# A hybrid diffusion step on one core: the gate's strips of two weight quarters put in a row, and the last norm's root taken from ScalarE's own sum

## The chip, the core and the metric

The kernel runs on one core of a Trainium2 chip. Its five engines work side by side, each through its own instructions in order: TensorE (PE, with its weight loads shown apart as PEld), VectorE (DVE), ScalarE (ACT), GpSimd (POOL) and SyncE (SP), whose queue here issues most of the DMA transfers. They wait for each other by semaphores. The metric is the device time of one execution in microseconds (us), the median of several runs.

## The reference

One layer of a diffusion trunk, in fp32, over 1024 latent tokens and 128 context tokens (nine tiles of 128 rows), 1024 wide:

```python
def _rmsnorm(x, g):
    y = x * lax.rsqrt(jnp.mean(x * x, axis=-1, keepdims=True) + EPS)
    return y * g
...
    mod = jax.nn.silu(cond) @ w_ada + b_ada
    shift, scale, gate = jnp.split(mod[:, None, :], 3, axis=-1)
    h = _rmsnorm(x, norm_g) * (1 + scale) + shift
    u, v, g_a, c_q, c_kv, k_rope, g_b = _split_in(h @ w_in)
    a_out = _chunk_mlp(u, v, w_s, b_s, g_v) * jax.nn.silu(g_a)
...
    y = jnp.concatenate([a_out, attn * jax.nn.silu(g_b)], axis=-1) @ w_o
    return x + gate * y
...
    y_prompt = _rmsnorm(xp, final_g)
    y_sample = _rmsnorm(xs, final_g)
```

Two places of it matter here: `gate`, the last third of the modulation (two conditions, latent and context, by 1024 columns, a product of two vectors of 1024 with a 1024 x 1024 part of w_ada, plus a bias), and the last `_rmsnorm`, of the ninth tile (the context tokens).

## The kernel before, in words

fp32 products are made of three passes over a high and a low part (fp32r) of each operand. The stages follow each other on PE almost without a gap: modulation and transposes; the wide input projection (u, g_a and g_b as six pairs n = 0 to 5 of column blocks, each pair in seven half-size products p1 to p7 by a Strassen-like scheme, and plain products tp of 24 matmuls for the third group of tokens); the narrow projection; attention; the output projection, also by such a scheme, in which the norm of each tile follows as its rows are done.

The order of the input projection's instructions comes from a small planner (class `Plan`): each step has an engine, a cost, what it depends on, a priority and resources, and the planner issues steps on a clock of its own. What it issues stands so on each engine; the time on the chip is then set by data and semaphores. A step on "D" issues DMAs on SP's queue.

The gate is made in the middle of this, at pair 3, in four quarters j of 256 columns (`gate_steps`):

- `ga{j}` fetches 1 MB of weights (`adag`, one buffer) and 2 KB of bias (`grow`).
- `gr{j}`, the strips: eight matmuls with 32 columns of weights (the two conditions and zeros), four of them side by side in four strips of the array, L1014. They write columns 0 to 255 of a PSUM bank `gps{j}` (`pst`, two banks).
- `gh{j}` and `gl{j}`: ScalarE takes the high part, DVE the low part.
- `gt{j}`, the sum: two small matmuls (L1026) add the four strips into columns 256 to 511 of the same bank.
- `go{j}`: DVE adds the bias, and SP writes the quarter to DRAM (`gdram`), from which the gate is loaded some 320 us later.

Where the strips and sums stand among PE's products is given by their dependencies on product steps, such as `"p3_2"`. Only when a quarter's strips are done may the next quarter's weights be fetched, as they share the buffer.

The last norm (`finish_left`) is that of tile 8, whose left half is PE's last product, in two parts of 256 columns. The squares of the right half and of the first part are summed early; `zv1` makes of them a mean with the epsilon. ScalarE squares the second part with an accumulated sum (`zq`); DVE joins the two (`zv`, L2327), ScalarE takes the root (`zr`, L2328), DVE makes minus a half of the mean square (`zw`, L2329), the reciprocal of the root (`zr0`) and a Newton step (`zr2`, `zr3`); then three engines scale the two halves and two DMAs write them. The small values lie in one PSUM bank, `smalls`.

Of the kernel before, what the change touches and what calls it, by code (L numbers as in the profile page):

```python
# [9 lines left out]
F32 = mybir.dt.float32  # L10
# [3 lines left out]
AF = mybir.ActivationFunctionType  # L14
ALU = mybir.AluOpType
# [3 lines left out]
P = 128  # L19
# [4 lines left out]
EPS = 1e-6  # L24
# [70 lines left out]
def tile_hymba_step(ctx: ExitStack, tc: tile.TileContext, I, O):  # L95
    nc = tc.nc
    V, S, G, T = nc.vector, nc.scalar, nc.gpsimd, nc.tensor

    def opened(name, bufs=1, space=None, side=None):
        kw = dict(name=name, bufs=bufs, reuse_waits="tile")  # L100
        if space is not None:
            kw["space"] = space
        if side is not None:
            kw["side"] = side
        cm = tc.tile_pool(**kw)
        return cm, cm.__enter__()
# [4 lines left out]
    def lo_of(lo, src, hi):  # L111
        V.tensor_tensor(lo, src, f32(hi), op=ALU.subtract)  # L112
# [58 lines left out]
    def catch_up(until):  # L171
        at_ = now[0]
        while waiting and waiting[0][0] <= until:
            due, fn = waiting.pop(0)
            now[0] = due
            fn()
        now[0] = at_
# [9 lines left out]
    def step(cost, fn):  # L187

        catch_up(now[0])
        for f in list(fill):  # L190
            if f[0] in made and made_at[f[0]] <= now[0]:
                fill.remove(f)
                run(f[1:])
        run((cost, fn))
# [12 lines left out]
    def run(step):  # L207
        catch_up(now[0])
        step[1]()
        now[0] += step[0]  # L210
# [16 lines left out]
    c_pc, pc = opened("pc", side="right")  # L227
    c_mx, mx = opened("mx", side="right")
    c_mc, mc = opened("mc", side="right")
    c_sm, sm = opened("sm", bufs=2, side="right")  # L230
    c_pt, pst = opened("pst", bufs=2, space=PSUM)
# [131 lines left out]
    ada = {}  # L363
# [276 lines left out]
    step = plan.add  # L640

    def bank(pool, tag, name):
        return pool.tile([P, 512], F32, tag=tag, name=name)
# [28 lines left out]
    def load_step(key, fn, deps, prio, cost=1.46):  # L672
        step(key, "D", cost, fn, deps, prio, lag=2.0)
# [81 lines left out]
    pools, opened_as = {}, {}  # L755
# [242 lines left out]
    def gate_steps(j):  # L998


        cell = {}
        prio = 8 + 0.1 * j

        def fetch():
            cell["w"] = pools["vg"].tile([P, 8, 256], F32, tag="ada", name=f"adag{j}")
            nc.sync.dma_start(cell["w"], I["ada_g"][j])
            cell["row"] = pools["vg"].tile([2, 256], F32, tag="row", name=f"grow{j}", bufs=2)
            nc.sync.dma_start(cell["row"], I["b_gate"][j : j + 1, :].rearrange("a (c r) -> (a c) r", c=2))

        def strips():  # L1010
            cell["ps"] = bank(pst, "t", f"gps{j}")
            for kk in range(NK):
                s_, i = kk % 4, kk // 4
                T.matmul(cell["ps"][32 * s_ : 32 * s_ + 32, 0:256], csp[:, kk, :], cell["w"][:, kk, :], start=i == 0, stop=i == 1)  # L1014

        def high():
            cell["hi"] = pools["vg"].tile([P, 256], F32R, tag="hig", name=f"hig{j}")
            S.copy(cell["hi"], cell["ps"][:, 0:256])

        def low():  # L1020
            cell["lo"] = pools["vg"].tile([P, 256], F32R, tag="log", name=f"log{j}")
            lo_of(cell["lo"], cell["ps"][:, 0:256], cell["hi"])

        def total():
            for m in range(2):
                T.matmul(cell["ps"][0:2, 256:512], selr, cell[("hi", "lo")[m]], start=m == 0, stop=m == 1)  # L1026

        def out():
            V.tensor_tensor(cell["row"], cell["ps"][0:2, 256:512], cell["row"], op=ALU.add)
            nc.sync.dma_start(gdram[:, 256 * j : 256 * j + 256], cell["row"])  # L1030

        load_step(f"ga{j}", fetch, ["vg", *([f"gr{j - 1}"] if j else [])], prio, cost=3.6)
        step(f"gr{j}", "T", 0.7, strips, [f"ga{j}", ("p3_2", "tp62", "p1_3", "p6_3")[j]], 4.0, takes=("pst",))
        step(f"gh{j}", "S", 0.4, high, [f"gr{j}"], 1.0)
        step(f"gl{j}", "V", 0.4, low, [f"gh{j}"], 1.0)
        step(f"gt{j}", "T", 0.35, total, [f"gl{j}", ("tp62", "p1_3", "p2_3", "p7_3")[j]], 4.0)
        step(f"go{j}", "V", 0.35, out, [f"gt{j}"], 1.0, gives=("pst",))

    def wide_weights():

# [78 lines left out]
    wuv = pc.tile([P, 4, P], F32, tag="wuv", name="wuv")  # L1119
# [444 lines left out]
    def pair_scores(i):  # L1564

        return score_steps(*heads[i]) if FROM <= i < UPTO else [s_ for h in range(2) for s_ in plain_steps(*heads[i + h])]
# [245 lines left out]
    with tc.manual_schedule(engines=engines):  # L1812
# [168 lines left out]
        first = pair_scores(0)  # L1981
# [76 lines left out]
    gate, ssq = {}, {}  # L2058
# [3 lines left out]
    step = plan.add  # L2062
    L, R = slice(0, 512), slice(512, 1024)

    def on_v(key, fn, deps, prio, cost=0.64, **kw):
        step(key, "V", cost, fn, deps, prio, lag=0.12, **kw)

    def on_s(key, fn, deps, prio, cost=0.6, **kw):
        step(key, "S", cost, fn, deps, prio, lag=0.15, **kw)
# [38 lines left out]
    def small(n):  # L2108
        c = used[0]
        used[0] += n  # L2110
        return smalls[:, c : c + n]
# [62 lines left out]
    for q in range(3, len(queue)):  # L2174
        n, name, _ = queue[q]
        cell = {}
# [16 lines left out]
    turn = [None]  # L2193
# [99 lines left out]
        product(2, first_banks[2], ks=[3])  # L2293

    def finish_left():
        v, v0, root, u, vn = (small(1) for _ in range(5))
        r = sm.tile([P, 1], F32, tag="fr", name="rlast")
        cell = {}
        fetch("own0", lambda: load_own(0, nc.sync.dma_start), ["y4"])
        g, x = (lambda: own[0][:, 0:512]), (lambda: own[0][:, 512:1024])  # L2300
        on_g("z4", lambda: G.tensor_tensor(keep, keep, fg[:, R], op=ALU.mult), ["sq8.1", "fg"], 2.5)

        cut_at = 256
        own_of = (slice(0, cut_at), slice(cut_at, 512))
        at_ = (slice(0, cut_at), slice(0, 512 - cut_at))

        def left(j):
            cell[j] = psw.tile([P, 512], F32, tag="w", name=f"left{j}")
            if j == 0:
                cell["junk"] = psw.tile([P, 512], F32, tag="w", name="junk")  # L2310
            out_terms(8, cell[j][:, at_[j]], own_of[j].start, own_of[j].stop, range(8))

        for j in range(2):
            o = lambda j=j: cell[j][:, at_[j]]
            dur = 0.43
            on_t(f"pz{j}", 2.9, lambda j=j: left(j), [], takes=("w",) if j else ("w", "w"))
            on_v(f"zm{j}", lambda o=o, c=own_of[j]: V.tensor_tensor(o(), o(), g()[:, c], op=ALU.mult), [f"pz{j}", "own0"], 0.5, dur)
            on_v(f"za{j}", lambda o=o, c=own_of[j]: V.tensor_tensor(o(), o(), x()[:, c], op=ALU.add), [f"zm{j}"], 0.5, dur)
        square(8, 0, lambda: cell["junk"][:, own_of[0]], L, ["za0"], 0.5, lambda: cell[0][:, own_of[0]])
        sums((8,), v0, 0.5)  # L2320
        on_v("zv1", lambda: V.tensor_scalar(v0, v0, 1.0 / 1024.0, EPS, op0=ALU.mult, op1=ALU.add), ["n8"], 0.5, 0.16)
        on_s(
            "zq", lambda: S.activation(cell["junk"][:, own_of[1]], cell[1][:, at_[1]], AF.Square, accum_out=ssq[(8,)][:, 2:3]), ["za1"], 0.4, 0.5
        )
        first, second = own_of
        on_v("zf", lambda: V.tensor_tensor(x()[:, first], cell[0][:, at_[0]], fg[:, first], op=ALU.mult), ["sq8.0", "fg"], 0.6, 0.43)
        on_v("zv", lambda: V.scalar_tensor_tensor(v, ssq[(8,)][:, 2:3], 1.0 / 1024.0, v0, op0=ALU.mult, op1=ALU.add), ["zq", "zv1"], 0.4, 0.2)  # L2327
        on_s("zr", lambda: S.activation(root, v, AF.Sqrt), ["zv"], 0.3, 0.25)  # L2328
        on_v("zw", lambda: V.tensor_scalar(vn, v, -0.5, None, op0=ALU.mult), ["zv"], 0.3, 0.16)  # L2329
        on_v("zr0", lambda: V.reciprocal(r, root), ["zr"], 0.2, 0.18)  # L2330
        on_v("zr2", lambda: V.scalar_tensor_tensor(u, r, r, vn, op0=ALU.mult, op1=ALU.mult), ["zr0", "zw"], 0.3, 0.18)
        on_v("zr3", lambda: V.scalar_tensor_tensor(r, u, 1.5, r, op0=ALU.add, op1=ALU.mult), ["zr2"], 0.3, 0.18)

        def out0():
            G.tensor_scalar(x()[:, first], x()[:, first], r, 0.0, op0=ALU.mult, op1=ALU.add)
            V.scalar_tensor_tensor(x()[:, second], cell[1][:, at_[1]], r, fg[:, second], op0=ALU.mult, op1=ALU.mult)
            nc.sync.dma_start(O["y"][8][:, L], x())

        def out1():
            S.activation(keep, keep, AF.Copy, scale=r)  # L2340
            nc.scalar.dma_start(O["y"][8][:, R], keep)

        on_v("zo0", out0, ["zr3", "zf"], 0.3, 0.6)
        on_s("zo1", out1, ["zr3", "z4"], 0.3, 0.6)
# [109 lines left out]
```

## Time and profile before

| what | value |
| --- | --- |
| runs | 602.42, 601.96, 602.82 us |
| median | 602.42 us |
| the profiled execution's own time | 602.15 us |
| its span, first to last instruction | 600.4 us |
| PE busy | 590.3 us (98%) |
| DVE, ACT, POOL busy | 427.3, 329.2, 214.0 us |
| mean granted TensorE clock | 0.997 |
| strips of the four quarters, starts on PE | 162.48, 170.21, 177.90, 185.62 us |

A row of a timeline has the start, the duration, the engine, the line, the operation, what it writes and reads, and a count; equal instructions in a row are merged. In brackets stands the idle time of the engine ahead of it and what ended it ("issue" is nothing that the profile shows). Matmuls overlap, so a merged row's duration reaches past the start of the next; a difference of starts is the time that a piece takes.

### The profile page before, as it was taken

The page shows a single profiled execution, that of the slowest core. Times are in us where ns is not written, and L with a number is a line of the kernel's source. Part 1 is how long each engine was busy: PE and PEld are TensorE (multiplying, and loading weights), DVE is VectorE, ACT ScalarE, POOL GpSimd, SP SyncE. Part 2 cuts the span into 40 slices and gives each one's busy share as a digit, 9 for nine tenths or more (in the row PEclk, how much of TensorE's full clock was granted, in tenths as well). Part 3 has the DMA queues.
Part 4 walks back from the last instruction along what each step waited for, and adds up shares of the span by engine and source line. Part 5 has one row for each costly group of instructions (what it writes and reads, how often), then busy time and mean ns, then how long its engine had stood idle before and what let it go on. Part 6 is the DMA issues. An engine that isn't in the chain of part 4 may idle for free.

```text
span 600.4 us, 10191 instructions
## 1 busy us (share of the span) xinstructions
PE 590.3 (98%) x3661; PEld 528.2 (88%) x3661; DVE 427.3 (71%) x940; ACT 329.2 (55%) x773; POOL 214.0 (36%) x251
## 2 busy tenths in 40 slices
PE   9999999999999999999999999999999999999995
PEld 8578889999989999999998888888888898888884
DVE  4666888977647368476678677778788876477885
ACT  6565886434323245465577566656656462457543
POOL 2571103200000000343363345454544547269834
PEclk9999999999999999999999999999999999999998
DMA  8991001032052134100002033434242029951444
GB/s 319 370 370 70 1 2 70 1 140 71 4 212 69 69 93 138 43 1 0 2 8 71 0 106 106 157 126 141 81 143 94 1 72 303 361 178 41 144 147 160
DMA packets 31059, 67.33 MB, mean 112 GB/s; under 512 B 3344, under 2 KB 17440, under 8 KB 29984
## 3 DMA queue, kind: packets, MB, share of 16 engines
q1 hardware_dynamic: 27792, 55.93, 26.9%
q0 software_dynamic: 2352, 8.39, 4.1%
q10 hardware_dynamic: 864, 2.36, 1.1%
q8 instruction: 29, 0.48, 0.3%
q14 instruction: 22, 0.18, 0.1%
HBM read 53.45 MB, written 13.21 MB: 111 GB/s over the span
## 4 chain that ended last, share of the span: by engine, by line
PE 93%; DMA 3%; DVE 2%; ACT 1%; POOL 1%; issue 0%; SPq 0%; POOLq 0%; ACTq 0%
PE p L916 14%; PE tp L937 7%; PE pT L1586 6%; PE o L1610 3%; PE o L1612 3%; PE o L1611 3%; PE zacc L1349 2%; PE zacc L1348 2%; PE zacc L1350 2%; PE S L1947 2%; PE S L1948 2%; PE S L1949 2%; DMA ada<-in_ada_ss 2%; PE s L1503 2%; PE s L1506 2%; PE s L1505 2%
## 5 line engine op out<-in xcount | busy, mean ns | idle before, releaser
L1463 POOL TENSOR_SCALAR e<-e,rs 128x1280 f32<-128x1280 f32 x32 | 47.0, 1468 | 97.2 <-DVE rs L1462 62.8
L112 DVE TENSOR_TENSOR pl<-pT,ph 128x512 fp32r<-128x512 f32 x81 | 55.5, 687 | 32.5 <-ACT ph L1590 32.2
L1458 ACT ACTIVATE e<-s,nb,scl 128x256 f32<-128x256 f32 x64 | 56.9, 890 | 38.9 <-DVE nb L1446 26.2
L1590 ACT CAST ph<-pT 128x512 fp32r<-128x512 f32 x80 | 47.1, 589 | 40.8 <-PE pT L1586 40.6
L1196 POOL TENSOR_TENSOR kr<-z,rope 128x64 f32<-128x64 f32 x8 | 2.6, 324 | 155.3 <-ACT z L1205 155.3
L937 PE MATMUL tp<-area,w 128*128 128x384 f32 x288 | 52.6, 338 | 0.0
L1610 PE MATMUL o<-ph,vh 128*128 128x256 f32 x160 | 50.7, 317 | 0.0
L937 PEld LDWEIGHTS tp<-area,w 128*128 128x128 f32 x288 | 50.4, 188 | 0.0
L1586 PE MATMUL pT<-ident,e 128*128 128x128 f32 x320 | 48.0, 273 | 0.0
L1586 PEld LDWEIGHTS pT<-ident,e 128*128 128x128 f32 x320 | 38.9, 140 | 7.2
L1612 PE MATMUL o<-ph,vl 128*128 128x256 f32 x160 | 45.1, 282 | 0.0
L1611 PE MATMUL o<-pl,vh 128*128 128x256 f32 x160 | 44.9, 280 | 0.0
L1440 DVE TENSOR_REDUCE m<-s 128x1 f32<-128x1024 f32 x32 | 39.0, 1218 | 2.6 <-PE s L1481 2.5
L1610 PEld LDWEIGHTS o<-ph,vh 128*128 128x128 f32 x160 | 30.2, 189 | 4.7 <-ACT os L1620 2.9
L1611 PEld LDWEIGHTS o<-pl,vh 128*128 128x128 f32 x160 | 30.4, 190 | 0.4
L1612 PEld LDWEIGHTS o<-ph,vl 128*128 128x128 f32 x160 | 30.1, 188 | 0.0
L916 PE MATMUL p<-area,w 128*128 128x384 f32 x144 | 27.7, 339 | 0.0
L916 PE MATMUL p<-area,s 128*128 128x384 f32 x144 | 27.3, 337 | 0.0
L1348 PE MATMUL zacc<-w1t,area 128*128 128x448 f32 x72 | 27.1, 376 | 0.0
L916 PE MATMUL p<-w1t,s 128*128 128x384 f32 x144 | 26.9, 339 | 0.0
L1349 PE MATMUL zacc<-w1t,area 128*128 128x448 f32 x72 | 26.3, 366 | 0.0
L1350 PE MATMUL zacc<-w1t,area 128*128 128x448 f32 x72 | 26.3, 365 | 0.0
(697 smaller groups left out, 1770.4 us busy)
## 6 DMA issues: line engine op xcount, KB each, us to landing
ada<-in_ada_ss SPq DMA_DIRECT2D x16, 512.0 KB, 6.0
w2r<-in_w_t SPq DMA_DIRECT2D x12, 512.0 KB, 5.1
x<-in_x SPq DMA_DIRECT2D x9, 512.0 KB, 8.4
adag<-in_ada_g SPq DMA_DIRECT2D x4, 1024.0 KB, 4.8
traw<-in_w_o SPq DMA_DIRECT2D x16, 256.0 KB, 3.8
tdram<-thi SPq DMA_DIRECT2D x32, 128.0 KB, 1.9
tdram<-traw SPq DMA_DIRECT2D x32, 128.0 KB, 1.8
wor<-in_w_o SPq DMA_DIRECT2D x8, 512.0 KB, 3.8
```

What stands on the lines that cost most here:

```text
L112: V.tensor_tensor(lo, src, f32(hi), op=ALU.subtract)
L916: T.matmul(banks[key], a_, b_, start=k == 0 and m == 0, stop=k == 3 and m == len(passes) - 1)
L937: T.matmul(tps[c, 2][:, :GW], w_[c][:, k, :], x_[k, 2], start=k == 0 and m == 0, stop=k == NK - 1 and m == 2)
L1348: T.matmul(ps[:, :448], a, wqh[k], start=k == 0, stop=False)
L1440: V.tensor_reduce(m[:, 0:1], lat_, axis=AX.X, op=ALU.max)
L1458: S.activation(e[:, sl], src, AF.Exp, bias=nb, scale=scl[:, t : t + 1], accum_out=su[:, i : i + 1])
L1463: G.tensor_scalar(e, e, rs, 0.0, op0=ALU.mult, op1=ALU.add)
L1586: T.transpose(ps[:, w : w + P], es[t, h][:, c * P : (c + 1) * P], ident)
L1590: later(0.5, lambda: S.copy(ph[:, :w], ps[:, :w]))
L1610: T.matmul(o, vh[:, kt, :], ph[:, sl], start=c == 0, stop=False)
L1611: T.matmul(o, vh[:, kt, :], pl[:, sl], start=False, stop=False)
L1612: T.matmul(o, vl[:, kt, :], ph[:, sl], start=False, stop=c == n - 1)
```

## The change

Two separate edits.

**The gate.** Quarters 0 and 1 get their strips directly behind each other in the middle of p1 of pair 3, quarters 2 and 3 behind the plain product of the same pair. For this the weights have two buffers, quarter j's being fetched when the strips of quarter j - 2 are done. The biases are fetched by a step of their own and lie in a shared tile (`grows`, in the slot that `wuv` uses later), two halves in turn. High, low, sum and output remain four each; the high part of the second quarter of a couple waits for the first one's sum, with which it shares a buffer.

**The last norm.** The share of the other columns with the epsilon goes into `rest8` in SBUF; the root is taken straight from ScalarE's accumulated sum, with `rest8` as bias. DVE makes minus a half of `rest8` ahead of time (`zv2`), and the half of the mean square from this and the accumulated sum (`zw`).

```diff
--- before.py
+++ after.py
@@ -1002,10 +1002,8 @@
         prio = 8 + 0.1 * j
 
         def fetch():
-            cell["w"] = pools["vg"].tile([P, 8, 256], F32, tag="ada", name=f"adag{j}")
+            cell["w"] = pools["vg"].tile([P, 8, 256], F32, tag="ada", name=f"adag{j}", bufs=2)
             nc.sync.dma_start(cell["w"], I["ada_g"][j])
-            cell["row"] = pools["vg"].tile([2, 256], F32, tag="row", name=f"grow{j}", bufs=2)
-            nc.sync.dma_start(cell["row"], I["b_gate"][j : j + 1, :].rearrange("a (c r) -> (a c) r", c=2))
 
         def strips():
             cell["ps"] = bank(pst, "t", f"gps{j}")
@@ -1013,6 +1011,12 @@
                 s_, i = kk % 4, kk // 4
                 T.matmul(cell["ps"][32 * s_ : 32 * s_ + 32, 0:256], csp[:, kk, :], cell["w"][:, kk, :], start=i == 0, stop=i == 1)
 
+        def bias():
+            if j == 0:
+                pools["rows"] = pc.tile([P, 512], F32, tag="wuv", name="grows")
+            cell["row"] = pools["rows"][0:2, 256 * (j % 2) : 256 * (j % 2) + 256]
+            nc.sync.dma_start(cell["row"], I["b_gate"][j : j + 1, :].rearrange("a (c r) -> (a c) r", c=2))
+
         def high():
             cell["hi"] = pools["vg"].tile([P, 256], F32R, tag="hig", name=f"hig{j}")
             S.copy(cell["hi"], cell["ps"][:, 0:256])
@@ -1029,12 +1033,19 @@
             V.tensor_tensor(cell["row"], cell["ps"][0:2, 256:512], cell["row"], op=ALU.add)
             nc.sync.dma_start(gdram[:, 256 * j : 256 * j + 256], cell["row"])
 
-        load_step(f"ga{j}", fetch, ["vg", *([f"gr{j - 1}"] if j else [])], prio, cost=3.6)
-        step(f"gr{j}", "T", 0.7, strips, [f"ga{j}", ("p3_2", "tp62", "p1_3", "p6_3")[j]], 4.0, takes=("pst",))
-        step(f"gh{j}", "S", 0.4, high, [f"gr{j}"], 1.0)
+        first = j % 2 == 0
+        load_step(f"ga{j}", fetch, ["vg", *([f"gr{j - 2}"] if j > 1 else [])], prio, cost=3.0)
+        load_step(f"gb{j}", bias, [f"ga{j}", *([f"go{j - 2}"] if j > 1 else [])], prio, cost=0.6)
+        turn = ["p3_2", "p1_3"][j // 2]
+        if first:
+            waits = [f"ga{j}", f"ga{j + 1}", turn, *(["go1"] if j else [])]
+            step(f"gr{j}", "T", 0.85, strips, waits, 4.0, takes=("pst",))
+        else:
+            step(f"gr{j}", "T", 0.95, strips, [f"|gr{j - 1}"], 0, takes=("pst",))
+        step(f"gh{j}", "S", 0.4, high, [f"gr{j}", *([] if first else [f"gt{j - 1}"])], 1.0)
         step(f"gl{j}", "V", 0.4, low, [f"gh{j}"], 1.0)
-        step(f"gt{j}", "T", 0.35, total, [f"gl{j}", ("tp62", "p1_3", "p2_3", "p7_3")[j]], 4.0)
-        step(f"go{j}", "V", 0.35, out, [f"gt{j}"], 1.0, gives=("pst",))
+        step(f"gt{j}", "T", 0.35, total, [f"gl{j}", ("tp62", "tp62", "p7_3", "p7_3")[j]], 4.0)
+        step(f"go{j}", "V", 0.35, out, [f"gt{j}", f"gb{j}"], 1.0, gives=("pst",))
 
     def wide_weights():
 
@@ -2293,8 +2304,9 @@
         product(2, first_banks[2], ks=[3])
 
     def finish_left():
-        v, v0, root, u, vn = (small(1) for _ in range(5))
+        v0, root, u, vn = (small(1) for _ in range(4))
         r = sm.tile([P, 1], F32, tag="fr", name="rlast")
+        rest_ = sm.tile([P, 1], F32, tag="fr", name="rest8")
         cell = {}
         fetch("own0", lambda: load_own(0, nc.sync.dma_start), ["y4"])
         g, x = (lambda: own[0][:, 0:512]), (lambda: own[0][:, 512:1024])
@@ -2318,15 +2330,15 @@
             on_v(f"za{j}", lambda o=o, c=own_of[j]: V.tensor_tensor(o(), o(), x()[:, c], op=ALU.add), [f"zm{j}"], 0.5, dur)
         square(8, 0, lambda: cell["junk"][:, own_of[0]], L, ["za0"], 0.5, lambda: cell[0][:, own_of[0]])
         sums((8,), v0, 0.5)
-        on_v("zv1", lambda: V.tensor_scalar(v0, v0, 1.0 / 1024.0, EPS, op0=ALU.mult, op1=ALU.add), ["n8"], 0.5, 0.16)
+        on_v("zv1", lambda: V.tensor_scalar(rest_, v0, 1.0 / 1024.0, EPS, op0=ALU.mult, op1=ALU.add), ["n8"], 0.5, 0.16)
+        on_v("zv2", lambda: V.tensor_scalar(v0, rest_, -0.5, None, op0=ALU.mult), ["zv1"], 0.55, 0.16)
         on_s(
             "zq", lambda: S.activation(cell["junk"][:, own_of[1]], cell[1][:, at_[1]], AF.Square, accum_out=ssq[(8,)][:, 2:3]), ["za1"], 0.4, 0.5
         )
         first, second = own_of
         on_v("zf", lambda: V.tensor_tensor(x()[:, first], cell[0][:, at_[0]], fg[:, first], op=ALU.mult), ["sq8.0", "fg"], 0.6, 0.43)
-        on_v("zv", lambda: V.scalar_tensor_tensor(v, ssq[(8,)][:, 2:3], 1.0 / 1024.0, v0, op0=ALU.mult, op1=ALU.add), ["zq", "zv1"], 0.4, 0.2)
-        on_s("zr", lambda: S.activation(root, v, AF.Sqrt), ["zv"], 0.3, 0.25)
-        on_v("zw", lambda: V.tensor_scalar(vn, v, -0.5, None, op0=ALU.mult), ["zv"], 0.3, 0.16)
+        on_s("zr", lambda: S.activation(root, ssq[(8,)][:, 2:3], AF.Sqrt, bias=rest_, scale=1.0 / 1024.0), ["zq", "zv1"], 0.3, 0.25)
+        on_v("zw", lambda: V.scalar_tensor_tensor(vn, ssq[(8,)][:, 2:3], -0.5 / 1024.0, v0, op0=ALU.mult, op1=ALU.add), ["zq", "zv2"], 0.3, 0.2)
         on_v("zr0", lambda: V.reciprocal(r, root), ["zr"], 0.2, 0.18)
         on_v("zr2", lambda: V.scalar_tensor_tensor(u, r, r, vn, op0=ALU.mult, op1=ALU.mult), ["zr0", "zw"], 0.3, 0.18)
         on_v("zr3", lambda: V.scalar_tensor_tensor(r, u, 1.5, r, op0=ALU.add, op1=ALU.mult), ["zr2"], 0.3, 0.18)
```

What this moves. PE at the second place, from the end of the plain product of pair 3 (`tp72`) on; `p6_3`, `p7_3`, `p5_3` are products of pair 3, `gps` the gate's banks. Before:

```order
L937 MATMUL tp72_1844<-area2_120,w271_1723 128x384
L916 MATMUL p6_3_1884<-w1t_121,s2_3_1670 128x384 x6
L1014 MATMUL gps2_1894<-adag2_1838,csp_110 32x256 x8
L916 MATMUL p6_3_1884<-w1t_121,s2_3_1670 128x384 x6
L916 MATMUL p7_3_1917<-w1t_121,s3_3_1782 128x384 x6
L1026 MATMUL gps2_1894<-hig2_1909,selr_651 2x256
L1026 MATMUL gps2_1894<-log2_1915,selr_651 2x256
L916 MATMUL p7_3_1917<-w1t_121,s3_3_1782 128x384 x6
L916 MATMUL p5_3_1938<-area1_119,s1_3_1703 128x384 x12
```

and now:

```order
L937 MATMUL tp72_1843<-area2_120,w271_1726 128x384
L1012 MATMUL gps2_1885<-adag2_1768,csp_110 32x256 x8
L1012 MATMUL gps3_1897<-adag3_1817,csp_110 32x256 x8
L916 MATMUL p6_3_1910<-w1t_121,s2_3_1673 128x384 x12
L916 MATMUL p7_3_1923<-w1t_121,s3_3_1773 128x384 x12
L916 MATMUL p5_3_1940<-area1_119,s1_3_1706 128x384 x6
L1030 MATMUL gps2_1885<-hig2_1906,selr_651 2x256
L1030 MATMUL gps2_1885<-log2_1908,selr_651 2x256
L916 MATMUL p5_3_1940<-area1_119,s1_3_1706 128x384 x6
```

The strips of quarter 3 came from the middle of `p4_3`; sum 2 moved behind, into `p5_3`, and sum 3 stands now in the middle of `p4_3`. At the first place, quarter 1's strips moved from behind sum 0 to directly behind quarter 0's.

SP's queue in the same stretch; `w2r4` to `w2r9` are the raw weights of pairs 2 to 4, `adag` and `grow` or `grows` the gate's weights and biases. Before:

```order
L1006 DMA adag0_1384<-in_ada_g 128x2048
L1008 DMA grow0_1386<-in_b_gate 2x256
L375 DMA w2r4_1425<-in_w_t 128x1024
L375 DMA w2r5_1441<-in_w_t 128x1024
L375 DMA w2r6_1588<-in_w_t 128x1024
L375 DMA w2r7_1592<-in_w_t 128x1024
L1006 DMA adag1_1762<-in_ada_g 128x2048
L1008 DMA grow1_1764<-in_b_gate 2x256
L375 DMA w2r8_1803<-in_w_t 128x1024
L375 DMA w2r9_1805<-in_w_t 128x1024
L1030 DMA gdram_91<-grow0_1386 2x256
L1006 DMA adag2_1838<-in_ada_g 128x2048
```

and now:

```order
L1006 DMA adag0_1384<-in_ada_g 128x2048
L375 DMA w2r4_1421<-in_w_t 128x1024
L375 DMA w2r5_1426<-in_w_t 128x1024
L1018 DMA grows_1441<-in_b_gate 2x256
L1006 DMA adag1_1446<-in_ada_g 128x2048
L1018 DMA grows_1441<-in_b_gate 2x256
L375 DMA w2r6_1591<-in_w_t 128x1024
L375 DMA w2r7_1595<-in_w_t 128x1024
L1006 DMA adag2_1768<-in_ada_g 128x2048
L375 DMA w2r8_1799<-in_w_t 128x1024
L375 DMA w2r9_1815<-in_w_t 128x1024
L1006 DMA adag3_1817<-in_ada_g 128x2048
```

The weights of quarters 1, 2 and 3 are each fetched one place earlier; those of quarter 3 now stand directly behind `w2r9`, ahead of the first write to `gdram`.

DVE at the end, from the addition of x to the last part on; `left1` is the last product's second part, `smalls` the PSUM bank of small values, `rlast` the norm's factor. Before:

```order
L2318 TENSOR_TENSOR left1_6666<-left1_6666,own0_6583 128x256
L2321 TENSOR_SCALAR smalls_6025<-smalls_6025 128x1
L2327 SCALAR_TENSOR_TENSOR smalls_6025<-fss8_6158,smalls_6025 128x1
L2329 TENSOR_SCALAR smalls_6025<-smalls_6025 128x1
L2330 RECIPROCAL rlast_6026<-smalls_6025 128x1
```

and now:

```order
L2330 TENSOR_TENSOR left1_6664<-left1_6664,own0_6581 128x256
L2333 TENSOR_SCALAR rest8_6024<-smalls_6022 128x1
L2334 TENSOR_SCALAR smalls_6022<-rest8_6024 128x1
L2341 SCALAR_TENSOR_TENSOR smalls_6022<-fss8_6156,smalls_6022 128x1
L2342 RECIPROCAL rlast_6023<-smalls_6022 128x1
```

The number of DVE's steps is the same. The step that reads ScalarE's sum (`fss8`) stood ahead of the root and made its operand; now it makes the half alone, and a step that needs nothing of the last part moved ahead of it.

## The prediction

> **What bounds the kernel now.** I read the page first, then TensorE's (PE's) waits, then the timeline of PE and of its weight loads (PEld) around the gate's strips, then the last microseconds of all engines. On the page, the span and the chain that ended last:
>
> ```profile
> span 600.4 us, 10191 instructions
> ...
> PE 93%; DMA 3%; DVE 2%; ACT 1%; POOL 1%; issue 0%; SPq 0%; POOLq 0%; ACTq 0%
> ```
>
> PE carries 93% of that chain. Its waits over the whole program (engine and line, what was waited for: us in total, times, longest):
>
> ```profile
> PE warm L442 <- DVE onesr L239: 1.4, 1, 1.4
> PE modp L337 <- DMA ada<-in_ada_ss: 0.6, 1, 0.6
> PE vacc L436 <- DVE area L112: 0.4, 1, 0.4
> PE w L1977 <- DVE kcl L112: 0.2, 1, 0.2
> ```
>
> The first three lines are of the opening stage; only the last, 0.2 us, lies behind the gate's strips. From there PE is one unbroken row of work: what is taken out of it at 163 to 190 us moves all that follows, up to the final norm, which hangs on PE's last product. So the change has two terms: what PE saves at the strips, and what the last chain saves.
>
> **The strips.** PE's timeline at strips 0 (start, us, operation, count; a strip matmul has two records, so x16 are eight):
>
> ```profile
> 161.35 1.21 PE L916 MATMUL p<-area,w 128*128 128x384 f32 x6
> 162.48 1.07 PE L1014 MATMUL gps<-adag,csp 128*32 128x256 f32 x16
> 163.48 1.32 PE L916 MATMUL p<-area,w 128*128 128x384 f32 x6
> 164.64 4.35 PE L937 MATMUL tp<-area,w 128*128 128x384 f32 x24
> 168.83 1.21 PE L916 MATMUL p<-area,w 128*128 128x384 f32 x6
> ```
>
> Twenty-four plain products take 168.83 - 164.64 = 4.19 us, so twelve take 2.09. The twelve of p1 with the strips among them take 164.64 - 161.35 = 3.29. One visit to the strips therefore costs 1.20 us. How much of that is work, and how much the price of a visit? The opening stage has the same strips in halves (weight loads; in brackets the idle time ahead and what ended it):
>
> ```profile
> 10.79 0.16 PEld L337 LDWEIGHTS modp<-ada,csp 128*32 128x32 f32 x8 [0.51 <-DMA ada<-in_ada_ss]
> 11.36 0.52 PEld L442 LDWEIGHTS warm<-ones,ident 128*128 128x128 f32 x4 [0.41 <-issue]
> ```
>
> and whole:
>
> ```profile
> 26.79 0.59 PEld L337 LDWEIGHTS modp<-ada,csp 128*32 128x32 f32 x16 [0.17 <-issue]
> 27.79 0.19 PEld L431 LDWEIGHTS vacc<-w1t,area 128*128 128x128 f32 x1 [0.41 <-issue]
> ```
>
> Four strip matmuls hold PE from 10.79 to 11.36, 0.57 us; eight from 26.79 to 27.79, 1.00 us. Four more cost 0.43, so eight more cost 0.86. A visit of 1.20 us is 0.86 of strips and 0.34 that is paid once, at the change from 128 columns to 32 and back. Before, there are four visits of eight matmuls; now two of sixteen. Saved: 2 x 0.34 = 0.68 us. The low end is nothing, if a seam between two sets costs what a visit does; the high end is rival one.
>
> That seam, the first strip of one quarter right behind the last of another in another PSUM bank, stands in no row. I take it at nothing, by the nearest row: plain products change bank and weights at every product without a step (p1, tp and p2 above follow each other in the pitch of 0.174 us that each has within). The Trainium skill, "TensorEngine Tiling (Array Packing)", Key Properties, says that changing the tiling mode drains TensorE, "not just tile". By that the seam, where the mode stays, would drain nothing; no run so far shows it.
>
> The two small matmuls that sum a quarter (L1026) remain four pairs:
>
> ```profile
> 174.44 0.28 PE L1026 MATMUL gps<-hig,selr 128*2 128x256 f32 x1
> 174.55 0.28 PE L1026 MATMUL gps<-log,selr 128*2 128x256 f32 x1
> 174.67 2.26 PE L937 MATMUL tp<-area,w 128*128 128x384 f32 x12
> ```
>
> A pair costs 174.67 - 174.44 = 0.23 us, wherever it stands among plain products.
>
> **What must be ready for it.** The new dues on PE: sets 0 and 1 from 162.5; sum 0 at 168.83 + six products (1.05) + 0.86 = 170.7; sum 1 at 174.44 - 0.34 = 174.1; set 2 at 174.67 + 2.09 - 0.34 = 176.4; set 3 about 1.0 later, 177.4; sum 2, behind both sets (2.06) and thirty products (5.24), at 183.7; sum 3 twelve products and a pair later, 186.0. What feeds set 3 goes over SP's queue:
>
> ```profile
> 163.61 0.33 SPq L1006 DMA_DIRECT2D adag<-in_ada_g  x1
> 163.99 0.28 SPq L1008 DMA_DIRECT2D grow<-in_b_gate  x1
> 164.41 1.26 SPq L375 DMA_DIRECT2D w2r<-in_w_t  x2
> ```
>
> A quarter's weights from issue to landing (KB each, median us):
>
> ```profile
> adag<-in_ada_g SPq DMA_DIRECT2D x4, 1024.0 KB, 4.8
> ```
>
> Weights 1 are now fetched behind w2r5, tens of us ahead of need. Weights 2 take the place that weights 1 had, at 163.6. Weights 3 are what is new in that stretch: they wait for set 1, and stand behind w2r8 and w2r9, so they are issued at 164.41 + 1.26 = 165.7 and land at 170.5 if nothing stands in the way. DVE read w2r9 at 173.03 without waiting (next rows), so 2 MB were through by then, and a third is through by 173.0 + 4.8 = 177.8 at the latest, 0.4 late. I take some 174, nearer to the row of 4.8, and so nothing; 0.4 goes into the range. DVE's rows that stand ahead of quarter 1's low half and total:
>
> ```profile
> 173.03 0.68 DVE L775 TENSOR_TENSOR sr<-w2r 128x512 f32<-128x512 f32 x1
> 173.63 1.22 DVE L112 TENSOR_TENSOR w<-w2r,w 128x1024 fp32r<-128x1024 f32 x1
> 174.87 0.41 DVE L1029 TENSOR_TENSOR grow<-gps,grow 2x256 f32<-2x256 f32 x1
> ```
>
> and the high and low halves of all quarters (ns min/median/max):
>
> ```profile
> L1018 ACT CAST hig<-gps x4: 372/373/374, 163.7 to 186.8; 128x256 fp32r<-128x256 f32 x4
> L112 DVE TENSOR_TENSOR log<-gps,hig x4: 419/425/425, 164.3 to 187.2; 128x256 fp32r<-128x256 f32 x4
> ```
>
> Sum 0 is out near 171.1; then DVE's total 0 (0.41), the sum of w2r9 (0.68) and low 1 (0.42) end near 172.6, against 174.1. Total 1, now behind w<-w2r (1.22), ends as before near 175.3; set 3 wants its bank at 177.4. Between sum 2 and sum 3 are 2.3 us for high 3 and low 3, 0.8 together, and some 0.5 for sum 2 to come out: 1 us to spare. PE's own products cover all three; what comes later than that costs PE as much. The bias rows and the writes to DRAM (2 KB each) have no reader near. On ScalarE and DVE a few steps of pair 2 change places by 1 us, with no due on PE within that.
>
> **The last chain.** From the last sum to the reciprocal:
>
> ```profile
> 594.15 0.16 DVE L2321 TENSOR_SCALAR smalls<-smalls 128x1 f32<-128x1 f32 x1
> 594.27 0.37 ACT L2323 ACTIVATE junk<-left 128x256 f32<-128x256 f32 x1 [1.57 <-DVE left L2318]
> 594.55 0.19 ACT L2323 ACTIVATION_READ_ACCUMULATOR junk<-left 128x1 f32 x1
> 594.78 0.17 DVE L2327 SCALAR_TENSOR_TENSOR smalls<-fss,smalls 128x1 f32<-128x1 f32 x1 [0.47 <-ACT junk L2323]
> 594.98 0.16 ACT L2328 ACTIVATE smalls<-smalls 128x1 f32<-128x1 f32 x1 [0.23 <-DVE smalls L2327]
> 595.16 0.17 DVE L2329 TENSOR_SCALAR smalls<-smalls 128x1 f32<-128x1 f32 x1 [0.22 <-ACT smalls L2328]
> 595.37 0.17 DVE L2330 RECIPROCAL rlast<-smalls 128x1 f32<-128x1 f32 x1
> ```
>
> Removed is DVE's sum L2327: 594.98 - 594.78 = 0.20 us. The root now follows ScalarE's own accumulator read and takes a bias. Such a root elsewhere, behind its read:
>
> ```profile
> 8.52 0.19 ACT L383 ACTIVATION_READ_ACCUMULATOR junk<-x 128x1 f32 x1
> 8.74 0.30 ACT L517 ACTIVATE xroot<-ssq,epsb 128x3 f32<-128x3 f32 x1
> ```
>
> and one with a bias on `smalls`:
>
> ```profile
> 591.02 0.21 ACT L2139 ACTIVATE smalls<-smalls,epsb 128x1 f32<-128x1 f32 x1
> ```
>
> The root starts 8.74 - 8.52 = 0.22 after the read began, as DVE's sum did (0.23): the step is gained whole. But a root with a bias takes 0.21 (source in PSUM) to 0.30 (all in SBUF) against 0.16; the new one reads SBUF and writes PSUM, so I take 0.25, 0.09 longer. Net 0.20 - 0.09 = 0.11 us (0.06 to 0.15). The new step of the other share (0.17, as L2329) runs behind L2321, by 594.5, ahead of the read's end at 594.74.
>
> By the diff the half (L2329, now L2341) could run beside the root, for 0.20 more. But in the row it begins only as the root ends, of which it reads nothing: both write `smalls`, one PSUM bank, and in both orders it waits for ScalarE. So it stays behind and I give nothing. The Trainium skill, "PSUM — Partial Sum Buffer", on PSUM bank collisions, forbids two engines on one bank and quadrant at once, other columns included, and wants a semaphore by bank: by that rule the 0.20 can't come while both lie in `smalls`. The row agrees.
>
> **Sum.** 0.68 + 0.11 = 0.79 us. The profiled execution took 602.15 us (its span 600.4): 602.15 - 0.79 = 601.36. It stands 0.27 under the median of the runs, 602.42, from which the same sum gives 601.63. I forecast 601.6 us, 0.13% faster. A measurement of this kernel can tell about 0.2% (1.2 us) from no change, so the likeliest outcome is "within 0.2%".
>
> **Rivals.** One: a visit costs all the weight loads' idle time around it.
>
> ```profile
> 162.48 0.59 PEld L1014 LDWEIGHTS gps<-adag,csp 128*32 128x32 f32 x16 [0.25 <-issue]
> 163.48 0.47 PEld L916 LDWEIGHTS p<-area,w 128*128 128x128 f32 x3 [0.41 <-issue]
> ```
>
> That is 0.25 + 0.41 = 0.66 per visit, two spared: 1.32, with the tail 1.43 us; 600.7 of the profiled time, 601.0 of the median. Against it: the half sets have the same 0.41, and four matmuls more cost 0.43, so strips still run in that idle time. Chance 0.12.
>
> Two: the seam costs as much as the visit that it replaces, or the 0.68 us are swallowed by a wait that PE does not have today. Only the tail's 0.11 is left: 602.04, or 602.3 of the median. For it: no row shows the seam. Against it: PE's one wait behind the strips is 0.2. Chance 0.16.
>
> Three, slower: set 3 stands at PE's head and waits for weights 3. From a landing at 177.4 each us late costs one; from 178.2 the kernel is slower than before, from 179.4 by over 0.2%. With a landing at 181: 602.15 - 0.79 + 3.6 = 605.0, or 605.2 of the median. For it: 3 MB now queue where 2 did. Against it: 181 is 15 us behind the issue, three times the median. Chance 0.06, of which 0.05 beyond 0.2%.
>
> **How the numbers follow.** The forecast has 0.66. The range runs from 600.9 (rival one, 601.0) to 602.5 (rival two, 602.3, with some scatter: the runs of before spread from 601.96 to 602.82); the 0.4 of late weights lies within it. Rival three is left out. Faster by over 0.2% means under 601.2: rival one, 0.12, and 0.08 of the forecast by scatter, 0.20. Slower: 0.05. Same: 0.75.
>
> **What would show it.** Right: two rows of 32 strip records, each some 1.86 us from its first load to the next plain one; the first product of pair 4 0.68 us earlier; the root 0.22 behind the start of the accumulator read, the half behind the root, the reciprocal 0.71 behind that start where it was 0.82. Wrong: a step between the two sets, a wait of PE at 170 to 187 us for weights, low halves or banks, or a new wait of PE behind 190.

## The result, and the profile after

The changed kernel takes 601.37 us (median of 22 runs, 600.74 to 602.41) where the kernel before takes 602.43 (22 runs in the same comparison): ratio 0.9983, 95% interval 0.9977 to 0.9989, so 1.06 us less (0.66 to 1.39). The forecast was 601.6, 0.79 less. The profiled execution took 601.43 us. Its page, span and chain, and PE's waits:

```profile
span 599.6 us, 10193 instructions
...
PE 91%; DMA 3%; DVE 2%; POOL 2%; ACT 1%; issue 1%; SPq 0%; POOLq 0%; ACTq 0%
```

```profile
PE warm L442 <- POOL ident masks.py:199: 1.4, 1, 1.4
PE modp L337 <- DMA ada<-in_ada_ss: 0.9, 2, 0.5
PE vacc L436 <- DVE area L112: 0.4, 1, 0.4
```

All three waits are of the opening stage: the change brought PE no new wait, the 0.2 us behind the strips is no longer in the list, and PE still carries most of the chain that ends last. Its weight loads at the two places where strips now stand (start, us; a strip has two records, so x32 are two sets of eight):

```profile
162.71 1.45 PEld L1012 LDWEIGHTS gps<-adag,csp 128*32 128x32 f32 x32 [0.25 <-issue]
164.57 0.99 PEld L916 LDWEIGHTS p<-area,w 128*128 128x128 f32 x6 [0.41 <-issue]
```

```profile
176.71 1.45 PEld L1012 LDWEIGHTS gps<-adag,csp 128*32 128x32 f32 x32 [0.25 <-issue]
178.58 1.51 PEld L916 LDWEIGHTS p<-w1t,s 128*128 128x128 f32 x9 [0.41 <-issue]
```

From the first strip load to the next plain one are 1.86 us at the first place and 1.87 at the second. One set took 1.00 before, and eight more strips were put at 0.86: the seam between the two sets costs nothing that can be seen.

To see what this is worth, take the same products in both traces. First further rows of PE's timeline before, from the first product of pair 4 (L916, in the timeline's first row) to the last product of the kernel, then the rows of after that answer to them, with p1 of pair 3 ahead (which stood at 161.35 before):

```profile
190.12 2.10 PE L916 MATMUL p<-area,w 128*128 128x384 f32 x11
...
207.08 2.28 PE L916 MATMUL p<-area,s 128*128 128x384 f32 x12
...
225.98 2.26 PE L916 MATMUL p<-area,s 128*128 128x384 f32 x12
...
593.02 0.28 PE L1978 MATMUL left<-area,ml 128*128 128x256 f32 x1
```

```profile
161.57 1.21 PE L916 MATMUL p<-area,w 128*128 128x384 f32 x6
...
189.62 2.28 PE L916 MATMUL p<-area,w 128*128 128x384 f32 x12
...
206.58 2.28 PE L916 MATMUL p<-area,s 128*128 128x384 f32 x12
...
225.38 2.26 PE L916 MATMUL p<-area,s 128*128 128x384 f32 x12
...
592.31 0.28 PE L1989 MATMUL left<-area,ml 128*128 128x256 f32 x1
```

The changed kernel is 0.22 us late at 161 (the opening stage, ahead of anything that the change touches) and 0.50 early at 190. The stretch with the strips is 0.72 us shorter; 0.68 was forecast. Nothing gives it back: 0.50 early at 207, 0.60 at 226, 0.71 at the last product. The 0.10 between 207 and 226, where both kernels run the same products, was in no step of mine; it comes up again below. The further 0.11 up to the last product comes from one place in the output projection, where PE wants a low part (`kcl`) from DVE, before and after:

```profile
504.24 0.50 PE L1977 MATMUL w<-kcl,area 128*128 128x512 f32 x1 [0.23 <-DVE kcl L112]
```

```profile
503.50 0.50 PE L1988 MATMUL w<-kcl,area 128*128 128x512 f32 x1
```

The product ahead of it starts at 503.53 before and at 502.95 after, so this step takes 0.71 us before and 0.55 now; other places give some hundredths back. It is the 0.2 us in the list of PE's waits before, to which the prediction gave no term.

The last chain, on ScalarE and DVE:

```profile
593.84 0.20 ACT L2336 ACTIVATION_READ_ACCUMULATOR junk<-left 128x1 f32 x1
594.07 0.26 ACT L2340 ACTIVATE smalls<-fss,rest 128x1 f32<-128x1 f32 x1
594.37 0.16 DVE L2341 SCALAR_TENSOR_TENSOR smalls<-fss,smalls 128x1 f32<-128x1 f32 x1 [0.58 <-ACT smalls L2340]
594.56 0.17 DVE L2342 RECIPROCAL rlast<-smalls 128x1 f32<-128x1 f32 x1
```

The root starts 0.23 behind the start of the read and takes 0.26 (forecast 0.22 and 0.25); the half (L2341) begins only behind the root, as forecast; the reciprocal starts 0.72 behind the read's start, where it was 0.82. The tail is worth 0.10 us.

### The profile page after: what moved, and what is told of

Same layout as the page of the kernel before. It is cut to its first block, busy times and chain, and to the rows that moved or that the text cites. A ratio compares the mean times of both kernels' runs of the same rounds, so it can differ in the third digit from the quotient of the medians.

```text
span 599.6 us, 10193 instructions
## 1 busy us (share of the span) xinstructions
PE 589.5 (98%) x3661; PEld 528.1 (88%) x3661; DVE 427.5 (71%) x940; ACT 329.9 (55%) x773; POOL 212.8 (35%) x251
## 4 chain that ended last, share of the span: by engine, by line
PE 91%; DMA 3%; DVE 2%; POOL 2%; ACT 1%; issue 1%; SPq 0%; POOLq 0%; ACTq 0%
PE p L916 14%; PE tp L937 7%; PE pT L1597 5%; PE o L1621 3%; PE o L1623 3%; PE o L1622 3%; PE zacc L1360 2%; PE zacc L1359 2%; PE zacc L1361 2%; PE S L1959 2%; PE S L1958 2%; PE S L1960 2%; PE s L1514 2%; PE s L1517 2%; DMA ada<-in_ada_ss 2%; PE s L1516 2%
## 5 line engine op out<-in xcount | busy, mean ns | idle before, releaser
L916 PE MATMUL p<-area,w 128*128 128x384 f32 x144 | 27.5, 337 | 0.0
L916 PE MATMUL p<-area,s 128*128 128x384 f32 x144 | 27.3, 337 | 0.0
L916 PE MATMUL p<-w1t,s 128*128 128x384 f32 x144 | 26.6, 339 | 0.0
```

What stands on the lines that cost most here:

```text
L916: T.matmul(banks[key], a_, b_, start=k == 0 and m == 0, stop=k == 3 and m == len(passes) - 1)
```

## Experiments

Four questions: what a visit to the strips costs and whether the two parts add up; what holds the half behind the root; what late weights cost; and, after the fourth run, what an address costs. "The change" below is the changed kernel. All comparisons are with the kernel before on the same chip; what is called so much above or below the change sets medians of two comparisons side by side (the kernel before took 602.38 to 602.50 us in them).

**The gate's half alone.** The last norm goes back to its old form:

```
- rest_ = sm.tile([P, 1], F32, tag="fr", name="rest8")
- zr: S.activation(root, ssq[(8,)][:, 2:3], AF.Sqrt, bias=rest_, scale=1/1024)
+ zv: V.scalar_tensor_tensor(v, ssq[(8,)][:, 2:3], 1/1024, v0, ...)
+ zr: S.activation(root, v, AF.Sqrt)
```

> The gate's half of the change alone (strips of two quarters in a row, last norm as before). My sum: two visits fewer at 0.34 us each, so 0.68 us under the kernel before in the same comparison (ratio 0.9989), the reciprocal of the last norm 0.82 us behind the start of the accumulator read. Rival one (a visit costs 0.66): 1.32 us under it (0.9978). Rival two (the seam costs what a visit costs): no difference (1.0000). Together with the run of the norm alone it also shows whether the 1.06 us measured for the whole change is more than its parts (0.79 by my sum).

Measured: 601.46 us (11 runs) against 602.38, ratio 0.9985 (0.9976 to 0.9993): 0.92 less. Its profiled execution was the slowest of the 11 (602.36), and two rows show why that says nothing against the change. The first products of pairs 3 and 4:

```profile
162.28 1.03 PE L916 MATMUL p<-area,w 128*128 128x384 f32 x5
...
190.33 1.93 PE L916 MATMUL p<-area,w 128*128 128x384 f32 x10
```

It was 0.93 late at pair 3 (162.28 against 161.35) from the opening stage, and 0.21 late at pair 4 (190.33 against 190.12): again 0.72 gained in between. Rival two (no difference) falls. By the median 0.92 lies between 0.68 and rival one's 1.32; the trace decides for 0.68.

**The norm's half alone.** The gate as before, the last norm as in the change.

> The last norm's half of the change alone (gate as before, four visits). My sum: 0.20 us of DVE's step less 0.09 to 0.10 for the longer root: 0.11 us under the kernel before (ratio 0.9998), not to be told from no change by the time; in the trace the reciprocal starts 0.71 us behind the start of the accumulator read (0.82 before) and the half begins behind the root's end. Rival: were the norm worth the 0.27 by which the measured gain exceeds my sum, the time would be 0.38 under and the reciprocal some 0.45 behind the read.

Measured: 602.16 us (11 runs) against 602.38, ratio 0.9998 (0.9989 to 1.0007); not to be told from no change. The read and the reciprocal:

```profile
595.04 0.19 ACT L2325 ACTIVATION_READ_ACCUMULATOR junk<-left 128x1 f32 x1
...
595.76 0.17 DVE L2331 RECIPROCAL rlast<-smalls 128x1 f32<-128x1 f32 x1
```

0.72 apart, as in the change. So what the median of the change shows beyond my 0.79 does not come from the norm.

**Eight visits.** The kernel before, each set cut in two:

```
- step(gr{j}, strips: kk 0..7, behind p3_2 / tp62 / p1_3 / p6_3)
+ step(gq{j}, strips: kk 0..3, behind p3_2 / tp62 / p1_3 / p6_3)
+ step(gr{j}, strips: kk 4..7, behind gq{j} and p1_3a / p2_3a / p6_3a / p4_3a)
```

> The kernel before with each quarter's eight strips cut into two sets of four, plain products between them: eight visits instead of four, the same work. My price of 0.34 us a visit: 4 x 0.34 = 1.36 us above the kernel before (ratio 1.0023), each half set 0.77 us from its first strip load to the next plain load, PE without a new wait. Rival one (0.66 a visit): 2.64 us above (1.0044), 1.09 us a half set. Rival two, read as that visits cost nothing by themselves: no difference (1.0000).

Measured: 603.63 us (11 runs) against 602.38, ratio 1.0020 (1.0011 to 1.0029): 1.25 more, PE without a new wait. The first half set among PE's weight loads, and two products of PE:

```profile
162.58 0.16 PEld L1015 LDWEIGHTS gps<-adag,csp 128*32 128x32 f32 x8 [0.25 <-issue]
163.15 0.99 PEld L916 LDWEIGHTS p<-area,w 128*128 128x128 f32 x6 [0.41 <-issue]
```

```profile
161.45 1.21 PE L916 MATMUL p<-area,w 128*128 128x384 f32 x6
...
208.51 2.28 PE L916 MATMUL p<-area,s 128*128 128x384 f32 x12
```

0.10 late at 161 and 1.43 late at 207 (208.51 against 207.08): 1.33 for four more visits, 0.33 each. That is the price of 0.34 from the other side, and rival one's 0.66 falls. (Load to load a half set takes 0.57, not the 0.77 that I wrote: 0.77 is the whole visit, of which some 0.2 lies ahead of its first load.)

**The root apart.** The change, with the root out of the PSUM tile `smalls`:

```
- v0, root, u, vn = (small(1) for _ in range(4))
+ v0, u, vn = (small(1) for _ in range(3))
+ root = sm.tile([P, 1], F32, tag="fq", name="root8", bufs=1)
```

> The changed kernel with the root of the last norm in an SBUF tile of its own instead of the PSUM tile of small values, so that the root (ScalarE) and the half (DVE) no longer write one PSUM bank. My theory (the half stands behind the root because of the shared bank): the half runs beside the root, the reciprocal starts 0.52 to 0.55 us behind the start of the accumulator read (0.71 in the changed kernel), some 0.17 us under the changed kernel and, with 0.79 for the change, 0.96 us under the kernel before (ratio 0.9984). If something else holds the half (the root being merely slow, or DVE's own queue): reciprocal still 0.71 behind, no difference to the changed kernel.

Measured: 602.04 us (11 runs), ratio 0.9996 (0.9987 to 1.0005): 0.67 above the change, where 0.17 less was expected. Yet the step did what I said:

```profile
594.40 0.19 ACT L2337 ACTIVATION_READ_ACCUMULATOR junk<-left 128x1 f32 x1
594.63 0.16 DVE L2342 SCALAR_TENSOR_TENSOR smalls<-fss,smalls 128x1 f32<-128x1 f32 x1 [0.29 <-ACT junk L2337]
594.63 0.29 ACT L2341 ACTIVATE root<-fss,rest 128x1 f32<-128x1 f32 x1
594.96 0.16 DVE L2343 RECIPROCAL rlast<-root 128x1 f32<-128x1 f32 x1 [0.16 <-ACT root L2341]
```

The half starts with the root, and the reciprocal 0.56 behind the read. So what they shared, one tile in one PSUM bank, had held it; no run parts the tile from the bank. What was lost, PE lost: its first product of pair 4 still stands ahead of the change, its last behind:

```profile
189.48 1.40 PE L916 MATMUL p<-area,w 128*128 128x384 f32 x7
...
592.87 0.28 PE L1989 MATMUL left<-area,ml 128*128 128x256 f32 x1
```

That is 0.14 early at 189 and 0.56 late (592.87 against 592.31) at the end. The new tile takes 32 bytes of each partition, and every tile of the pools opened after it, the attention's among them, lies 32 bytes lower. The next runs test that.

**The root in a tile that was there.** The tile of the other share gets a second column for the root, and no address changes:

```
+ two = sm.tile([P, 2], F32, tag="fr", name="rest8")
+ rest_, root = two[:, 0:1], two[:, 1:2]
```

> The changed kernel with the root out of the shared PSUM bank, as in the run before, but as second column of the SBUF tile that holds the other share: no tile in SBUF changes its address. (The tile of its own moved all tiles of the attention by 32 bytes.) My theory: the reciprocal 0.56 us behind the start of the accumulator read as there, the matmuls of the attention at the changed kernel's pace, so 0.15 us under the changed kernel: 601.2 us (ratio to the kernel before 0.9980). Rival: what slowed the attention was the root itself, or chance of that build: near 602.0 again (0.9996).

Measured: 601.16 us (11 runs, 600.90 to 601.55) against 602.45, ratio 0.9980 (0.9971 to 0.9989). The reciprocal is 0.55 behind the read:

```profile
593.71 0.19 ACT L2337 ACTIVATION_READ_ACCUMULATOR junk<-left 128x1 f32 x1
...
594.26 0.16 DVE L2343 RECIPROCAL rlast<-rest 128x1 f32<-128x1 f32 x1 [0.16 <-ACT rest L2341]
```

It has the lowest median of this study. That it beats the change is shown in the chain (0.17 less); the two medians, 0.21 apart, were taken in different comparisons and their intervals overlap.

**An address alone.** The change, and the tile of the other share takes 32, 64 or 128 bytes of its own; besides the tiles behind it only the last norm's two small tiles (`rest8`, `rlast`) change their place:

```
- rest_ = sm.tile([P, 1], F32, tag="fr", name="rest8")
+ rest_ = sm.tile([P, n], F32, tag="fq", name="rest8", bufs=1)[:, 0:1]    (n = 1, 16, 32)
```

> The changed kernel with nothing changed but an address: the tile of the other share gets 32 bytes of its own, by which the tiles of the attention lie 32 bytes lower, as in the run with the root apart. The last norm stays as in the changed kernel (reciprocal 0.71 us behind the read). By the theory that the address makes the attention's matmuls slower: 0.6 to 0.8 us above the changed kernel, 602.1 us (ratio to the kernel before 0.9995), the loss between 240 and 480 us. By the rival (the address is nothing): 601.4 (0.9983).

> The same with 64 bytes instead of 32: the tiles of the attention lie 64 bytes lower, at the same place within 64 bytes as in the changed kernel. If the place within 64 bytes decides: as the changed kernel, 601.4 us (ratio to the kernel before 0.9983). If any move does it: as with 32 bytes, 602.1 (0.9995).

> The changed kernel with the attention's tiles 128 bytes lower, nothing else (32 cost 0.64 us of the median, 64 cost 0.49). If the address counts by its place within 128 bytes: no loss, 601.4 us (ratio to the kernel before 0.9983). If it counts against tiles that did not move, whatever the step: some 0.5 us lost, 601.9 (0.9992).

Measured: 602.01, 601.86 and 602.95 us (11 runs each; ratios 0.9995, 0.9992 and 1.0008), so 0.64, 0.49 and 1.58 above the change. By the intervals only the 128 bytes are clear of the change (0.9999 at the lowest against 0.9989 at its highest); for the others the traces decide. The first product of pair 4 and the last product of the kernel, with 32 bytes:

```profile
190.12 0.69 PE L916 MATMUL p<-area,w 128*128 128x384 f32 x3
...
593.51 0.28 PE L1989 MATMUL left<-area,ml 128*128 128x256 f32 x1
```

Between them lie 403.39 us, where the change has 592.31 - 189.62 = 402.69: 0.70 lost. The same stretch takes 403.39 in the run with the root apart too, 403.36 with 64 bytes, 404.39 with 128, and 402.70 with the root in a tile that was there. So the theory of the address holds, both theories of a period (64 or 128 bytes) fall, and the size of the loss (0.70, 0.67 and 1.70) follows no rule that I can give. Two groups of the attention's matmuls between 360 and 480 us, in the change and with 32 bytes, and one of them with 128 and in the kernel before (count, then busy us and mean ns of one):

```profile
L1597 PE MATMUL pT<-ident,e 128*128 128x128 f32 x206 | 31.0, 272 | 0.0
...
L1515 PE MATMUL s<-kcl,area 128*128 128x512 f32 x39 | 15.2, 388 | 0.0
```

```profile
L1597 PE MATMUL pT<-ident,e 128*128 128x128 f32 x200 | 30.0, 272 | 0.0
...
L1515 PE MATMUL s<-kcl,area 128*128 128x512 f32 x40 | 15.8, 394 | 0.0
```

```profile
L1515 PE MATMUL s<-kcl,area 128*128 128x512 f32 x39 | 15.4, 394 | 0.0
```

```profile
L1504 PE MATMUL s<-kcl,area 128*128 128x512 f32 x40 | 15.6, 389 | 0.0
```

These score products are 6 ns longer each, without a wait and at a granted clock of 1.00, while the transposes keep their 272. That is some 0.24 us for 40 of them, only a part of the loss, and it is the same with 32 and with 128 bytes; the rest is spread over other groups. Why the address counts stays open. The change itself has no part in this: it leaves the attention's tiles where the kernel before had them, and its score products take 388 ns against 389.

**Late weights.** The change, with weights 3 issued later: behind quarter 1's write to DRAM, or behind quarter 2's bias row:

```
  fetch(3):   - nc.sync.dma_start(cell["w"], I["ada_g"][3])
  out(1):     + nc.sync.dma_start(adag3, I["ada_g"][3])      (first run)
  bias(2):    + nc.sync.dma_start(adag3, I["ada_g"][3])      (second run)
```

> The changed kernel with one transfer issued later: weights 3 go out on SP's queue only behind the second quarter's write to DRAM (about 175.4 us) instead of at 166.0. Nothing else on the queue by then, so by the row of 4.8 us they land near 180.3, where set 3 is due at 176.72 + 0.93 = 177.65. Rival three's price (what comes late on PE is paid one for one, nothing gives it back): PE waits some 2.7 us in front of set 3, and the kernel is as much slower than the changed one: near 604.1 us, 1.7 above the kernel before (ratio 1.003). If PE's later work had slack that swallows it: the wait in the trace, and no difference in the time.

Measured: 606.06 us (4 runs) against 602.45, ratio 1.0059 (1.0045 to 1.0073): 4.7 above the change, with one wait of 2.85. PE around it, and what clock it was granted (us of the stretch, PE busy, clock, DMA share, GB/s):

```profile
180.84 1.94 PE L1016 MATMUL gps<-adag,csp 128*32 128x256 f32 x16 [2.85 <-DMA adag<-in_ada_g]
...
182.70 5.00 PE L916 MATMUL p<-w1t,s 128*128 128x384 f32 x24
```

```profile
179.00:181.00 2.00, 0.16 (x4) 0.87 0.49 206
181.00:183.00 2.00, 2.00 (x17) 0.50 0.03 8
183.00:185.00 2.00, 2.00 (x10) 0.78 0.00 0
185.00:187.00 2.00, 2.00 (x13) 1.00 0.00 0
```

The same 24 products in the change:

```profile
178.58 4.43 PE L916 MATMUL p<-w1t,s 128*128 128x384 f32 x24
```

Set 3 takes 182.70 - 180.84 = 1.86 us instead of 1.00, the 24 products 0.57 more: the granted clock was 0.87, 0.50 and 0.78 in the stretches from 179 to 185. In finer stretches it is 1.00 up to 180.4, 0.50 from 180.5 to 183.8 and 1.00 again from 183.9: a half for some 3.4 us, and it fell while PE was still waiting. The Trainium skill, "TensorE: Matmul & The Clock Gate", Part 1, puts the halving behind an idle window of about 3.4 us; here 2.85 us were enough. So a wait of 2.85 costs 2.85 + 0.86 + 0.57 = 4.28, and 0.2 more that the next run shows alone. Nothing gives it back: the last product is 4.66 late, 0.20 of it from the opening stage.

> As the run with late weights 3, but issued earlier, behind the bias row of quarter 2 (near 174.2 us instead of 175.7). There they landed 5.1 us after the issue, so here near 179.3, and set 3, due at 177.65, waits some 1.6 us. By the theory that a wait is paid one for one: 1.6 us above the changed kernel, 603.0 (ratio to the kernel before 1.001). By the theory that every wait of this size also costs the clock, at the rate of the other run (4.5 us lost for 2.85 waited): 2.5 us, 603.9 (1.0024), and a granted clock well under 1 for some 4 us behind the wait. By the theory that only a wait beyond a bound between 1.6 and 2.85 us costs the clock: 603.0 with the clock at 1.00 throughout.

Measured: 602.03 us (10 runs) against 602.50, ratio 0.9992 (0.9983 to 1.0001): 0.66 above the change. The bias row went out at 172.81 and not at 174, so the weights were issued at 173.15 and the wait was only 0.41:

```profile
176.57 1.07 PE L1016 MATMUL gps<-adag,csp 128*32 128x256 f32 x16
178.05 1.07 PE L1016 MATMUL gps<-adag,csp 128*32 128x256 f32 x16 [0.41 <-DMA adag<-in_ada_g]
179.05 4.43 PE L916 MATMUL p<-w1t,s 128*128 128x384 f32 x24
```

```profile
178.00:180.00 2.00, 1.95 (x21) 1.00 0.04 9
```

The clock stays at 1.00, and the 24 products keep their 4.43. From the first strip to the next plain product are 179.05 - 176.57 = 2.48 us instead of 1.86: 0.62 for a wait of 0.41. The other 0.21 goes with stopping and starting again; the rows don't part it further. Where between 0.41 and 2.85 us the clock begins to fall was not found.

## Why the prediction was right, point by point

**What bounds the kernel.** Right. PE is one row of work from the strips to the end; what was taken out at 163 to 179 was still there at the last product. The one wait in that row, 0.2 us, was seen and given no term (see the sum).

**The strips, 2 x 0.34 = 0.68.** Right in mechanism and size: 0.72 in the trace of the change and in that of its gate half, 0.33 a visit with four visits more. The split into 0.86 of work and 0.34 of visit, taken from the opening stage's half and whole sets, holds.

**The seam at nothing.** Right: 1.86 us for two sets where 1.00 + 0.86 were forecast. With it rival two falls.

**The dues.** Right: sum 0 stands at 170.92, sum 1 at 174.29, set 2 at 176.72, sum 2 at 183.89 and sum 3 at 186.22, where I wrote 170.7, 174.1, 176.4, 183.7 and 186.0; they are 0.2 to 0.3 later, of which 0.22 is the opening stage. The weights of quarter 3 were there by 174, as I took it: the DMA engines were busy for 0.85 of the stretch from 168 to 174 us and for 0.01 of that from 174 to 180. No wait formed.

**The tail, 0.11.** Right: 0.10, by the steps given. The 0.20 that I gave nothing for is there once the root leaves `smalls`: the reciprocal came 0.16 to 0.17 earlier, not 0.20, since such a root takes 0.29 instead of 0.26.

**The sum, 0.79.** Too small by a fourth. The two terms of it measured 0.72 and 0.10 in the trace; two pieces that it lacks come on top. 0.10 comes between 207 and 226, where the same products run some 1 ns faster each. The trace of the gate half has it too (0.21 late at 207, 0.10 at 226); those of the norm half (0.43 late at both) and of the eight visits (1.43 and 1.44) don't. It goes with the new order of the gate, and why is open. 0.11 comes from the shorter wait at 504. That one isn't shown to be the change's doing: the norm half still has a wait of 0.2 there, but the eight visits, with the gate's order of before, have none either. 1.03 in all, against 1.06 by the medians (0.66 to 1.39).

**Rival three.** Didn't happen, but I had its price wrong: "each us late costs one" measured 0.62 for 0.41 and 4.5 for 2.85. A landing at 180.84 gave 606.06 us, where I had put 605.2 for one at 181.

## What to carry to other kernels

Where one engine works without a pause, count the changes of shape in its queue, not only its work: here two fewer were worth 0.7 us, and the price could be read from rows that had the same work in two sizes. Before a transfer is moved closer to its due, price its lateness with the clock behind it. And when a small edit adds a tile, look first at whether its addresses moved other tiles: 32 to 128 bytes cost between 0.5 and 1.6 us here, from half of what the whole change gained to half as much again.

## What the runs showed of the hardware that I had not expected

- With a wait of PE of 2.85 us the granted clock falls to 0.50, for some 3.4 us from the end of the wait on, and all in all it costs 4.5 us; one of 0.41 keeps the clock at 1.00 and costs 0.62 (one profiled execution each).
- The same attention matmuls take 388 or 394 ns by where their tiles lie in SBUF (32, 64 and 128 bytes lower: 0.64, 0.49 and 1.58 us in the kernel's time).
- The opening stage, the same code in all, differs between executions by up to some 1.0 us (p1 of pair 3 at 161.25, with 128 bytes, to 162.28, in the gate half), and PE carries that to the end; one profiled execution is therefore compared stretch by stretch, not by its span.
